# A hybrid mLSTM and convolution step: order of the decode queries, the state update, the next head's scores and the weight split

## The chip, the core and the metric

The kernel runs on one core of a Trainium2 chip. The time is the device time of one execution in microseconds (us). The engines are named as in the profile: PE is TensorE (matrix products), PEld its weight loads, DVE is VectorE, ACT is ScalarE, POOL is GpSimd and SP is SyncE, which here only issues DMAs. Each engine runs its own instructions in the order in which the program lists them, and waits for the others by semaphores.

## What is computed

One layer of a decoder in float32: 512 new tokens of a prompt and 8 samples of 8 tokens each, with width 2048. One projection feeds an mLSTM with four heads of 256 and a convolution group of 1024 channels; a second projection joins them, with a residual and a layer norm. The samples have a state each, 8 matrices C of 256 x 256 per head.

```python
proj = jnp.einsum('bsd,de->bse', x, w_in) + b_in
q, k, v, o, zm, ga, gg, zc, ig, fg = jnp.split(proj, SPLITS, axis=-1)
...
num = (w_inter[..., None] * jnp.einsum('bhtd,bhde->bhte', qc, C)
       + jnp.einsum('bhts,bhse->bhte', s, vc))
...
C_new = decay[..., None, None] * C + jnp.einsum('bhs,bhsd,bhse->bhde', ws, kc, vc)
...
out = jnp.einsum('bse,ed->bsd', mix, w_out)
y = _layernorm(DN_ALPHA * x.astype(jnp.float32) + out.astype(jnp.float32))
```

So the queries of the samples meet the old states C (first einsum of `num`), and the states are updated from the keys and values (`C_new`). The two are independent of each other but for C itself, which the update overwrites in place.

## The kernel before, in words

The projection is the backbone. It is cut into 61 steps (s = 4 to 64), one for every 128 output columns that are made there; a step has 16 slices (k) of 128 inputs, and a k is six matmuls: 576 tokens in two halves of 256 and 320 columns, times three products (whi by xh, whi by xl, wlo by xh) that together give float32 precision. Weights come in units of four k. A DMA brings 512 KB into a `raw` tile (two units); `split` (L77 to L91) makes from each unit a rounded part `whi` on ScalarE (L86) and the rest `wlo` on VectorE (L87). Both have RING = 4 tiles. In the main loop `split(u + RING - 1)` is called as unit u begins, so that three units stand ahead, and whi must wait until PE has left unit u - 1.

All other work is put beside the projection by a table: `at(s, k, f, ...)` lists what is emitted behind the matmuls of step s, slice k (a k of 16 or more runs on into the next step). Since every engine runs in order, this table fixes the order on each of them. For each head h, with b = 6 h + 1, these are, in order of the stage:

- `b_E` (L428 to L447): masks on POOL (L444), then exponentials on ScalarE (L439).
- `b_parts` (L455, L456) splits q and k in two; `b_QK` (L468 to L479) makes the scores; `b_rep`, `b_kT` (L502 to L507) and `b_stk` transpose k and lay it out for the samples; `b_q` (L482 to L492) lays the queries out in Q, in three bfloat16 parts. `b_vT` and what follows do the same for v.
- `c_split` (L379 to L407) cuts four states of the samples, one after the other, in three bfloat16 parts c0, c1, c2: c0 (L401) and c1 (L399) on ScalarE, the remainders cr (L407) and c2 (L404) on VectorE. It is done for two halves r of the 8 samples.
- `b_sKV(h, r)` (L646 to L658) makes four products of keys and values on PE (L652) and adds them to the decayed states in place on VectorE (L657); POOL sends each state out (`o_cs`, L658). `b_qC(h, r)` (L633 to L644) multiplies Q by the parts of the states (L640). `c_next` loads the next head's states into the tiles that are free.
- `b_sLN` (L664 to L680): part 0 is a product of the samples' own scores and values (L667), part 1 gathers the results of qC, part 2 adds them (L679) and calls `head_ln` (L600 to L622), whose root is two small activations (L594, L595). `b_shT` transposes the result.

Products of this side work share three PSUM tiles, `mi`, which are given out in turn: sKV takes all three and one more, and whoever comes next has to wait until VectorE has read one. For the projection there are other PSUM tiles (`pp`). At each step's end `evac` takes the step's result to SBUF (L201 to L203 for q, k, v).

In the convolution (steps after head 3's) VectorE adds 31 taps per channel (L766) for the prompt and reduces a window for the samples (L776, L778). The output projection (L1045 to L1080) takes its weights through the same ring.

Of the kernel before, what the change touches and what calls it, by code (L numbers as in the profile page):

```python
# [9 lines left out]
BF16 = mybir.dt.bfloat16  # L10
# [4 lines left out]
P = 128  # L15
# [29 lines left out]
NU_IN = 4 * len(ORDER)  # L45
NU_OUT = 56
NU_LAST = 8
NU = NU_IN + NU_OUT
RING = 4
EOFF = [0, 512, 896, 1152]  # L50
PAIRS = [(i, j) for i in range(4) for j in range(i + 1)]
CW = 410
# [4 lines left out]
def hybrid(ctx, tc, x0, wg0, wu, wgate, cpack, gpack, sct, hist, xres, lnp,  # L57
# [7 lines left out]
    def mt(shape, dt, name, tag=None, bufs=None):  # L65
        return main.tile(shape, dt, name=name, tag=tag or name, bufs=bufs or 1)
# [49 lines left out]
    hT = {}  # L116
# [150 lines left out]
    for k in range(KT):  # L267
        for n, x in enumerate((XH, XL)):
            for b in range(2):
                c0, c1 = SPANS[b]  # L270
                pe.matmul(pg[b][:40, :c1 - c0], lhsT=WG[k // 8][:, k % 8], rhs=x[k // 2][:, k % 2, c0:c1],
                          start=k == 0 and n == 0, stop=k == KT - 1 and n == 1)
    for n in range(3):
        split(n)
    G = [gt([40, TOK], F32R, n) for n in ("Gh", "Gl")]
    for ps, (c0, c1) in zip(pg, SPANS):
# [93 lines left out]
    m = {}  # L370
# [8 lines left out]
    def c_split(h, r, j, part):  # L379

        i = NB * h + 4 * r
        if (j, part) == (0, 0):
            if (h, r) == (0, 1):
                for n in ("c0", "c1"):
                    m[n] = [mt([P, 2, 2, 258], BF16, n, tag="hT", bufs=8) for _ in range(2)]
            else:
                for n, tag in (("c0", "Ph"), ("c1", "Pl")):
                    c = m["t"]([P, 4, 2, 258], BF16, n, tag=tag)  # L390
                    m[n] = [c[:, :2], c[:, 2:]]
            c = m["t"]([P, 4, 2, 258], BF16, "c2")
            m["c2"] = [c[:, :2], c[:, 2:]]
            m["cr"] = {}
        c0, c1, c2 = (lambda j, c=m[n]: c[j // 2][:, j % 2] for n in ("c0", "c1", "c2"))
        cr = m["cr"]
        if part == 0:
            if j:
                act.activation(c1(j - 1), cr[j - 1], AF.Copy)  # L399
            if j < 4:  # L400
                act.activation(c0(j), CS[i + j], AF.Copy)  # L401
        else:
            if j:
                dve.tensor_sub(c2(j - 1), cr.pop(j - 1), c1(j - 1))  # L404
            if j < 4:
                cr[j] = m["t"]([P, 2, 258], F32, "cr", bufs=2)
                dve.tensor_sub(cr[j], CS[i + j], c0(j))  # L407
# [285 lines left out]
    def at(s, k, f, *a):  # L693
        s, k = s + k // KT, k % KT
        beside.setdefault((s, k), []).append((f, a))
# [5 lines left out]
    for h in range(NH):  # L701
        b = 6 * h + 1
        o = 2 if h == 0 else 0
        for i in range(4):
            at(b + 3 + o, (14 + i if h == 0 else 7 + 2 * i), b_E, h, i)
        at(6 if h == 0 else b + 2, 11 if h == 0 else 5, b_parts, "q", h)
        at(6 if h == 0 else b + 4, 13 if h == 0 else 0, b_parts, "k", h)
        at(b + 4 + o, 5, b_QK, h, 0)
        at(b + 4 + o, 7, b_QK, h, 1)
        at(b + 4 + o, 7, b_rep, "k", h)  # L710
        at(b + 4 + o, 9, b_kT, h, 0)
        at(b + 4 + o, 11, b_kT, h, 1)
        at(b + 4 + o, 13, b_stk, "k", h)
        at(b + 4 + o, 14, b_q, h)
        if h + 1 < NH:
            at(b + 7, 0, rb_load, h + 1)
        o = 14 if h == 0 else 0
        at(b + 6, o + 1, b_rep, "v", h)
        at(b + 6, o + 2, b_vT, h, 0)
        at(b + 6, o + 4, b_vT, h, 1)  # L720
        at(b + 6, o + 6, b_stk, "v", h)
        at(b + 6, o + 7, b_vs, h)
        at(b + 6, o + 9, b_sn, h)
        o = (b + 6, o + 10)
        for I in range(4):
            at(o[0], o[1] + 2 * I, b_SV, h, I)
        at(o[0], o[1] + 7, lambda h: head_ln(m["num"], P, 4, CT[:, 14:18, h]), h)
        at(o[0], o[1] + 8, b_KV, h, 0)
        at(o[0], o[1] + 10, b_KV, h, 1)
        at(o[0], o[1] + 14, b_hT, h, 0)  # L730
        at(o[0], o[1] + 16, b_hT, h, 1)
        for r, k in enumerate((8, 30 if h == 0 else 29)):
            for j in range(5):
                for part in range(2):
                    at(o[0], o[1] + k + 4 * j + 2 * part, c_split, h, r, j, part)
            at(o[0], o[1] + (24, 49 if h == 0 else 46)[r], b_sKV, h, r)
            at(o[0], o[1] + (28, 51)[r], b_qC, h, r)
            at(o[0], o[1] + (33, 55)[r], c_next, h, r)
        at(o[0], o[1] + 26, b_sLN, h, 0)
        at(o[0], o[1] + 57, b_sLN, h, 1)  # L740
        at(o[0], o[1] + 66, b_sLN, h, 2)
        at(o[0], o[1] + 76, b_shT, h)


    cv = {}
# [170 lines left out]
    c0 = FIRST + ORDER.index(("zc", 0))  # L916
    c1 = c0 + 2
# [16 lines left out]
    for n_, (n, e) in enumerate(ORDER):  # L934
        s = FIRST + n_
        pp = pp_tile()
        outs = halves(pp[:, 0], pp[:, 1])
        for k in range(KT):
            u = 4 * n_ + k // 4
            if k % 4 == 0:  # L940
                split(u + RING - 1)
            w = slice((k % 4) * P, (k % 4 + 1) * P)
            proj(outs, WHI[u][:, w], WLO[u][:, w], k)
            for f, a in beside.pop((s, k), []):
                f(*a)
        evac(n, e, outs)
# [106 lines left out]
                (act if c0 > 1536 else nc.sync).dma_start(out[:, c0:c0 + 512 // n], zc)  # L1053

    blocks = [(0, 512), (512, 512), (1024, 512), (1536, 256), (1792, 256)]
    u, nxt = NU_IN, NU_IN + RING - 1
    act.preload_act_table_set("natural_log_exp_and_others")
    for bi, (c0, w) in enumerate(blocks):
        kpu = 512 // w
        pst = wo_tiles(bi)  # L1060
        if bi < 4:
            for un in range(KT // kpu):
                for _ in range(2):
                    if nxt < NU and nxt <= u + RING - 1 or NU <= nxt < NU + NU_LAST:
                        split(nxt)
                        nxt += 1
                mix_next(2)
                if bi < 2 and un > 1 and extra:
                    nc.sync.dma_start(*extra.pop(0))
                for kk in range(kpu):  # L1070
                    kt = un * kpu + kk
                    hi, lo = (W[u][:, kk * w:(kk + 1) * w] for W in (WHI, WLO))
                    for t in range(5):
                        wmm(pst[t][:, :w], t, kt, hi, lo)
                u += 1
            later = [evac_z(t, pst[t], c0, w) for t in range(5)]
            while bi == 3 and nxt < NU + NU_LAST:
                split(nxt)
                nxt += 1
            for f in later:  # L1080
                f()
        else:
            for t in (4, 0, 1, 2, 3):
                for kt in range(KT):
                    hi, lo = (W[:, kt * w:(kt + 1) * w] for W in lastw)
                    wmm(pst[t][:, :w], t, kt, hi, lo)
                f = evac_z(t, pst[t], c0, w)
                f()
                ln_ops(t)
# [58 lines left out]
```

## Time and profile before

| | |
|---|---|
| time, median of 3 runs | 1145.81 us (1145.46 to 1146.2) |
| the profiled execution | 1146.47 us |
| its span | 1144.8 us |
| mean granted TensorE clock | 0.992 |
| PE busy | 1120.3 us (98%) |
| PEld busy | 1072.1 us (94%) |
| DVE busy | 740.9 us (65%) |
| ACT busy | 424.4 us (37%) |
| POOL busy | 148.6 us (13%) |

The span is the time from the first to the last instruction that the profiler saw; the execution's own time has a little around it. Busy shares are means over stages that differ: ScalarE and VectorE are half idle over the whole program, and can still be late in one place. Where a row of the timeline ends in brackets, the engine was idle for the first number of us just before, and the name is that of the instruction that ended it. A granted clock of 1.00 is 2.4 GHz, and 0.5 would be 1.2 GHz all through.

### The profile page before, as it was taken

How to read it: one execution, taken by the hardware profiler on the slowest of the kernel's cores; microseconds unless marked ns; L12 is line 12 of the kernel's file. 1: busy time of each engine (PE TensorE's matmuls, PEld its weight loads, DVE VectorE, ACT ScalarE, POOL GpSimd, SP SyncE). 2: the span in 40 equal slices, each digit the busy share in tenths (PEclk: the TensorE clock that was granted, in tenths of full speed). 3: DMA queues.
4: the chain of work that ended last, by engine and by line, in shares of the span. 5: the costliest groups of instructions: out<-in, count | busy, mean ns of one | idle time of the engine just before them, and what ended most of it. 6: DMA issues, size and time to landing. Idle time of an engine off the chain costs nothing.

```text
span 1144.8 us, 19958 instructions
## 1 busy us (share of the span) xinstructions
PE 1120.3 (98%) x8126; PEld 1072.1 (94%) x8126; DVE 740.9 (65%) x1250; ACT 424.4 (37%) x813; POOL 148.6 (13%) x217
## 2 busy tenths in 40 slices
PE   9999999999999998999999999999999999999996
PEld 8999998989999997999999999999999988888896
DVE  6385555555465545527899898999977871433448
ACT  5335553454445454422222222221336661221224
POOL 0021021021021002200011111111203310000004
PEclk9999999999999998999999999999999999999998
DMA  8114244244235222332233223222232245542228
GB/s 292 68 56 160 84 142 146 79 145 146 74 113 197 80 66 93 110 108 92 84 107 102 90 85 100 75 74 92 79 107 74 77 156 186 199 153 94 65 93 166
DMA packets 45228, 129.09 MB, mean 113 GB/s; under 512 B 5660, under 2 KB 11164, under 8 KB 44688
## 3 DMA queue, kind: packets, MB, share of 16 engines
q1 hardware_dynamic: 38880, 113.11, 29.6%
q0 software_dynamic: 4992, 12.94, 4.3%
q10 hardware_dynamic: 1264, 1.78, 0.5%
q8 instruction: 63, 1.03, 0.4%
q14 instruction: 29, 0.24, 0.1%
HBM read 110.91 MB, written 19.78 MB: 114 GB/s over the span
## 4 chain that ended last, share of the span: by engine, by line
PE 60%; DVE 1%; issue 0%; DVEq 0%
PE pp L185 42%; PE pp L1020 3%; PE pp L1021 3%; PE pp L1019 3%; PE mi L1020 2%; PE mi L1021 2%; PE mi L1019 2%; PE mi L1016 1%; PE mi L1015 1%; PE ns L1021 0%; PE ns L1019 0%; PE ns L1020 0%; DVE Ct L657 0%; DVE z L1052 0%; DVE c L404 0%; DVE z L1040 0%
## 5 line engine op out<-in xcount | busy, mean ns | idle before, releaser
L185 PE MATMUL pp<-xh,whi 128*128 128x256 f32 (+1 forms) x1952 | 422.8, 298 | 0.0
L185 PE MATMUL pp<-xl,whi 128*128 128x256 f32 (+1 forms) x1952 | 416.6, 295 | 0.0
L185 PE MATMUL pp<-xh,wlo 128*128 128x256 f32 (+1 forms) x1952 | 416.2, 295 | 0.0
L87 DVE TENSOR_TENSOR wlo<-raw,whi 128x512 fp32r<-128x512 f32 x300 | 220.8, 740 | 278.6 <-ACT whi L86 278.4
L185 PEld LDWEIGHTS pp<-xh,whi 128*128 128x128 f32 x1952 | 324.0, 189 | 5.2 <-issue 3.7
L185 PEld LDWEIGHTS pp<-xh,wlo 128*128 128x128 f32 x1952 | 327.6, 189 | 0.0
L185 PEld LDWEIGHTS pp<-xl,whi 128*128 128x128 f32 x1952 | 327.3, 189 | 0.0
L86 ACT ACTIVATE whi<-raw 128x512 fp32r<-128x512 f32 x300 | 187.6, 631 | 335.3 <-PE pp L185 175.8
L766 DVE SCALAR_TENSOR_TENSOR Y<-U,cp,Y 128x512 f32<-128x512 f32 x240 | 189.7, 790 | 5.3
L1020 PE MATMUL pp<-whi,mx 128*128 128x512 f32 (+1 forms) x128 | 46.9, 366 | 0.0
L1019 PE MATMUL pp<-whi,mx 128*128 128x512 f32 (+1 forms) x128 | 46.9, 366 | 0.0
L1021 PE MATMUL pp<-wlo,mx 128*128 128x512 f32 (+1 forms) x128 | 46.9, 366 | 0.0
L658 POOL DMA_DIRECT2D o_cs<-Ct x32 | 22.7, 779 | 170.8 <-DVE Ct L657 170.6
L1020 PE MATMUL mi<-whi,mx 128*128 128x512 f32 (+1 forms) x96 | 36.1, 376 | 0.0
L1019 PE MATMUL mi<-whi,mx 128*128 128x512 f32 (+1 forms) x96 | 36.0, 375 | 0.0
L1021 PE MATMUL mi<-wlo,mx 128*128 128x512 f32 (+1 forms) x96 | 36.0, 375 | 0.0
L399 ACT ACTIVATE c<-cr 128x516 bf16<-128x516 f32 x32 | 20.2, 632 | 42.0 <-DVE cr L407 42.0
L799 ACT ACTIVATE sg<-pp,cp 128x256 f32<-128x256 f32 (+1 forms) x48 | 21.3, 495 | 38.3 <-PE pp L185 38.2
L1021 PEld LDWEIGHTS pp<-wlo,mx 128*128 128x128 f32 x128 | 24.1, 188 | 4.3
L1019 PEld LDWEIGHTS pp<-whi,mx 128*128 128x128 f32 x128 | 24.0, 188 | 4.3
L1020 PEld LDWEIGHTS pp<-whi,mx 128*128 128x128 f32 x128 | 24.0, 188 | 4.3
L1047 POOL DMA_DIRECT2D o_ys<-zs x4 | 3.4, 1182 | 188.9 <-ACT zs L1046 188.9
(340 smaller groups left out, 1378.6 us busy)
## 6 DMA issues: line engine op xcount, KB each, us to landing
raw<-wu SPq DMA_DIRECT2D x154, 512.0 KB
Ct<-sct SPq DMA_DIRECT2D x32, 258.0 KB
o_cs<-Ct POOLq DMA_DIRECT2D x32, 256.0 KB, 3.2
xr<-x SPq DMA_DIRECT2D x16, 288.0 KB
z<-xres SPq DMA_DIRECT2D x8, 512.0 KB
wr<-wg SPq DMA_DIRECT2D x16, 192.0 KB
o_y<-z POOLq DMA_DIRECT2D x11, 256.0 KB, 7.0
o_y<-lnp SPq DMA_DIRECT2D x2, 1024.0 KB
```

The source lines that it names most:

```text
L86: act.activation(hi, r, AF.Copy)
L87: (eng or dve).tensor_tensor(out=lo, in0=r, in1=hi, op=OP.subtract)
L185: pe.matmul(out[b], lhsT=w, rhs=x[:, slice(*SPANS[b])], start=k == 0 and n < 2, stop=k == KT - 1 and n >= 4)
L399: act.activation(c1(j - 1), cr[j - 1], AF.Copy)
L658: pool.dma_start(o_cs[NB * h + b], c)
L766: dve.scalar_tensor_tensor(y, u, w, y, op0=OP.mult, op1=OP.add)
L799: act.activation(sg[:, c0:c1], ps, AF.Sigmoid, bias=b_in[:, c:c + 1])
L1015: pe.matmul(ps, lhsT=s_, rhs=hi, start=first, stop=False)
L1016: pe.matmul(ps, lhsT=s_, rhs=lo, start=False, stop=last)
L1019: pe.matmul(ps, lhsT=h_, rhs=hi, start=first, stop=False)
L1020: pe.matmul(ps, lhsT=l_, rhs=hi, start=False, stop=False)
L1021: pe.matmul(ps, lhsT=h_, rhs=lo, start=False, stop=last)
```

## The change

The numbers of the `at` table and the lead of the weight split are changed; no instruction of arithmetic is added or taken away.

- `LEAD = RING - 2`: units are split two ahead, at the start, in the main loop and in the output projection. RING stays 4.
- The order in each half r of the states was sKV, then qC, then c_next. It is now qC (21 k behind the first part of c_split), sKV (23) and c_next (27). For heads above 0 the second c_split begins one k later. The three parts of sLN move by one k, shT too.
- For h = 1 the group parts(k), QK, rep(k), kT, stk(k), q is emitted 16 to 17 k later, for h = 2 and 3 it is 4 k later.
- `c_split(0, 1)` uses the tiles Ph and Pl, as the other calls do, and two tiles of its own are gone.

```diff
@@ -47,6 +47,7 @@
 NU_LAST = 8
 NU = NU_IN + NU_OUT
 RING = 4
+LEAD = RING - 2
 EOFF = [0, 512, 896, 1152]
 PAIRS = [(i, j) for i in range(4) for j in range(i + 1)]
 CW = 410
@@ -270,7 +271,7 @@
                 c0, c1 = SPANS[b]
                 pe.matmul(pg[b][:40, :c1 - c0], lhsT=WG[k // 8][:, k % 8], rhs=x[k // 2][:, k % 2, c0:c1],
                           start=k == 0 and n == 0, stop=k == KT - 1 and n == 1)
-    for n in range(3):
+    for n in range(LEAD):
         split(n)
     G = [gt([40, TOK], F32R, n) for n in ("Gh", "Gl")]
     for ps, (c0, c1) in zip(pg, SPANS):
@@ -379,16 +380,11 @@
     def c_split(h, r, j, part):
 
 
-
         i = NB * h + 4 * r
         if (j, part) == (0, 0):
-            if (h, r) == (0, 1):
-                for n in ("c0", "c1"):
-                    m[n] = [mt([P, 2, 2, 258], BF16, n, tag="hT", bufs=8) for _ in range(2)]
-            else:
-                for n, tag in (("c0", "Ph"), ("c1", "Pl")):
-                    c = m["t"]([P, 4, 2, 258], BF16, n, tag=tag)
-                    m[n] = [c[:, :2], c[:, 2:]]
+            for n, tag in (("c0", "Ph"), ("c1", "Pl")):
+                c = m["t"]([P, 4, 2, 258], BF16, n, tag=tag)
+                m[n] = [c[:, :2], c[:, 2:]]
             c = m["t"]([P, 4, 2, 258], BF16, "c2")
             m["c2"] = [c[:, :2], c[:, 2:]]
             m["cr"] = {}
@@ -704,14 +700,15 @@
         for i in range(4):
             at(b + 3 + o, (14 + i if h == 0 else 7 + 2 * i), b_E, h, i)
         at(6 if h == 0 else b + 2, 11 if h == 0 else 5, b_parts, "q", h)
-        at(6 if h == 0 else b + 4, 13 if h == 0 else 0, b_parts, "k", h)
-        at(b + 4 + o, 5, b_QK, h, 0)
-        at(b + 4 + o, 7, b_QK, h, 1)
-        at(b + 4 + o, 7, b_rep, "k", h)
-        at(b + 4 + o, 9, b_kT, h, 0)
-        at(b + 4 + o, 11, b_kT, h, 1)
-        at(b + 4 + o, 13, b_stk, "k", h)
-        at(b + 4 + o, 14, b_q, h)
+        at(6 if h == 0 else b + 4, 13 if h == 0 else 17 if h == 1 else 4, b_parts, "k", h)
+        o = 16 * o + (0, 16, 4, 4)[h]
+        at(b + 4, o + 5, b_QK, h, 0)
+        at(b + 4, o + 7, b_QK, h, 1)
+        at(b + 4, o + 7, b_rep, "k", h)
+        at(b + 4, o + 9, b_kT, h, 0)
+        at(b + 4, o + 11, b_kT, h, 1)
+        at(b + 4, o + 13, b_stk, "k", h)
+        at(b + 4, o + 14, b_q, h)
         if h + 1 < NH:
             at(b + 7, 0, rb_load, h + 1)
         o = 14 if h == 0 else 0
@@ -729,17 +726,17 @@
         at(o[0], o[1] + 10, b_KV, h, 1)
         at(o[0], o[1] + 14, b_hT, h, 0)
         at(o[0], o[1] + 16, b_hT, h, 1)
-        for r, k in enumerate((8, 30 if h == 0 else 29)):
+        for r, k in enumerate((8, 30)):
             for j in range(5):
                 for part in range(2):
                     at(o[0], o[1] + k + 4 * j + 2 * part, c_split, h, r, j, part)
-            at(o[0], o[1] + (24, 49 if h == 0 else 46)[r], b_sKV, h, r)
-            at(o[0], o[1] + (28, 51)[r], b_qC, h, r)
-            at(o[0], o[1] + (33, 55)[r], c_next, h, r)
-        at(o[0], o[1] + 26, b_sLN, h, 0)
-        at(o[0], o[1] + 57, b_sLN, h, 1)
-        at(o[0], o[1] + 66, b_sLN, h, 2)
-        at(o[0], o[1] + 76, b_shT, h)
+            at(o[0], o[1] + k + 21, b_qC, h, r)
+            at(o[0], o[1] + k + 23, b_sKV, h, r)
+            at(o[0], o[1] + k + 27, c_next, h, r)
+        at(o[0], o[1] + 25, b_sLN, h, 0)
+        at(o[0], o[1] + 58, b_sLN, h, 1)
+        at(o[0], o[1] + 67, b_sLN, h, 2)
+        at(o[0], o[1] + 77, b_shT, h)
 
 
     cv = {}
@@ -938,7 +935,7 @@
         for k in range(KT):
             u = 4 * n_ + k // 4
             if k % 4 == 0:
-                split(u + RING - 1)
+                split(u + LEAD)
             w = slice((k % 4) * P, (k % 4 + 1) * P)
             proj(outs, WHI[u][:, w], WLO[u][:, w], k)
             for f, a in beside.pop((s, k), []):
@@ -1053,7 +1050,7 @@
                 (act if c0 > 1536 else nc.sync).dma_start(out[:, c0:c0 + 512 // n], zc)
 
     blocks = [(0, 512), (512, 512), (1024, 512), (1536, 256), (1792, 256)]
-    u, nxt = NU_IN, NU_IN + RING - 1
+    u, nxt = NU_IN, NU_IN + LEAD
     act.preload_act_table_set("natural_log_exp_and_others")
     for bi, (c0, w) in enumerate(blocks):
         kpu = 512 // w
@@ -1061,7 +1058,7 @@
         if bi < 4:
             for un in range(KT // kpu):
                 for _ in range(2):
-                    if nxt < NU and nxt <= u + RING - 1 or NU <= nxt < NU + NU_LAST:
+                    if nxt < NU and nxt <= u + LEAD or NU <= nxt < NU + NU_LAST:
                         split(nxt)
                         nxt += 1
                 mix_next(2)
```

The first place is VectorE from the end of c_split(0, 0) on, in step 10. L657 is the update of sKV (L653 after the change), L404 makes c2 (L400), L407 makes cr (L403), L87 is wlo (L88). Before:

```order
L87 TENSOR_TENSOR wlo<-raw,whi 128x512
L657 SCALAR_TENSOR_TENSOR Ct<-Ct,dec,mi 128x2x256 x3
L657 SCALAR_TENSOR_TENSOR Ct<-Ct,dec,ns 128x2x256
L404 TENSOR_TENSOR c_1719<-cr,c_1718 128x516
L87 TENSOR_TENSOR wlo<-raw,whi 128x512 x2
L407 TENSOR_TENSOR cr<-Ct,c_1987 128x516
L87 TENSOR_TENSOR wlo<-raw,whi 128x512
L404 TENSOR_TENSOR c_1991<-cr,c_1989 128x516
L407 TENSOR_TENSOR cr<-Ct,c_1987 128x516
```

and after the change:

```order
L88 TENSOR_TENSOR wlo<-raw,whi 128x512
L400 TENSOR_TENSOR c_1713<-cr,c_1712 128x516
L88 TENSOR_TENSOR wlo<-raw,whi 128x512
L653 SCALAR_TENSOR_TENSOR Ct<-Ct,dec,mi 128x2x256 x3
L653 SCALAR_TENSOR_TENSOR Ct<-Ct,dec,ns 128x2x256
L88 TENSOR_TENSOR wlo<-raw,whi 128x512
L403 TENSOR_TENSOR cr<-Ct,c_1963 128x516
L88 TENSOR_TENSOR wlo<-raw,whi 128x512
L400 TENSOR_TENSOR c_1965<-cr,c_1964 128x516
```

The update stood ahead of the last c2 of the first half; it now stands behind it, next to the first cr of the second half.

The second place is ScalarE at the end of step 12 after the change, from kT of head 1 to the evacuation of v. There kwh is the transposed and weighted k, sm the root of head norm in sLN(0, 2), hi the replicated k, Q the queries. The same part for head 1 in the kernel before (at the end of step 11):

```order
L506 ACTIVATE kwh<-mi,CT 128x256 x2
L642 ACTIVATE nsb<-mi 128x258
L644 DMA nsd_719<-nsb 128x516
L506 ACTIVATE kwh<-mi,CT 128x256 x2
L86 ACTIVATE whi<-raw 128x512
L542 ACTIVATE hi<-mi,WSs 128x256 x2
L489 ACTIVATE Q<-qw 128x16x8
L491 ACTIVATE Q<-qw 128x16x8
L203 ACTIVATE v<-pp,cp 128x256
L203 ACTIVATE v<-pp,cp 128x320
```

and after the change:

```order
L502 ACTIVATE kwh<-mi,CT 128x256 x2
L590 ACTIVATE sm_2437<-sm_2437 64x1
L591 ACTIVATE sm_2437<-sm_2437 64x1
L502 ACTIVATE kwh<-mi,CT 128x256 x2
L87 ACTIVATE whi<-raw 128x512
L538 ACTIVATE hi<-mi,WSs 128x256 x2
L485 ACTIVATE Q<-qw 128x16x8
L487 ACTIVATE Q<-qw 128x16x8
L204 ACTIVATE v<-pp,cp 128x256
L204 ACTIVATE v<-pp,cp 128x320
```

Before, the small activations of sLN(0, 2) came later, behind the evacuation of v; now they stand between the second and the third kwh, and what follows them is the end of step 12, not of step 11. The qC result (nsb) is gone from between the kwh.

## Rows read from the trace of the kernel before

**Rows 1.** The page, part 1: each engine's busy time, share of the span, instructions.

```profile
PE 1120.3 (98%) x8126; PEld 1072.1 (94%) x8126; DVE 740.9 (65%) x1250; ACT 424.4 (37%) x813; POOL 148.6 (13%) x217
```

**Rows 2.** What PE waits for, whole span: us in total, times, longest us.

```profile
PE mi L667 <- DVE Ct L657: 6.4, 3, 4.8
PE mi L640 <- DVE c L404: 3.1, 5, 1.2
```

**Rows 3.** Timeline of PE at three gaps: start us, us, row, [idle before <-releaser].

```profile
176.92 0.66 PE L502 MATMUL mi<-ident,k 128*128 128x128 f32 x4 [2.37 <-DVE Ct L657]
...
439.11 1.12 PE L667 MATMUL mi<-vs,Es 64*64 64x258 f32 x2 [4.82 <-DVE Ct L657]
...
465.00 0.52 PE L640 MATMUL mi<-c,Q 128*32 128x258 bf16 x12 [1.17 <-DVE c L404]
```

**Rows 4.** Stretches behind two gaps: us, then busy PE, PEld, DVE, ACT, POOL; PEclk, DMA.

```profile
175.00:184.00 9.00, 7.08 (x61) 6.40 (x62) 5.36 (x10) 2.47 (x6) 3.46 (x6) 0.81 0.76 237
436.00:444.00 8.00, 4.89 (x34) 3.71 (x38) 6.24 (x8) 1.53 (x3) 4.06 (x5) 0.57 0.58 196
```

**Rows 5.** The convolution: a stretch of 20 us; timelines of DVE and PE.

```profile
780.00:800.00 20.00, 20.00 (x154) 20.00 (x153) 19.61 (x26) 3.95 (x7) 1.42 (x1) 1.00 0.24 83
...
804.56 0.68 DVE L87 TENSOR_TENSOR wlo<-raw,whi 128x512 fp32r<-128x512 f32 x1
...
845.74 2.70 DVE L87 TENSOR_TENSOR wlo<-raw,whi 128x512 fp32r<-128x512 f32 x3 [0.94 <-ACT whi L86]
...
876.20 1.57 DVE L87 TENSOR_TENSOR wlo<-raw,whi 128x512 fp32r<-128x512 f32 x1 [1.33 <-ACT whi L86]
...
802.64 0.42 PE L185 MATMUL pp<-xh,whi 128*128 128x256 f32 x2
...
843.72 0.42 PE L185 MATMUL pp<-xh,whi 128*128 128x256 f32 x2
```

**Rows 6.** Head 0 to head 1: timelines of PE, DVE, POOL, ACT; L468 alone, 165 to 174.

```profile
147.32 0.39 PE L652 MATMUL mi<-vS,kS 32*128 32x256 f32 x3
...
155.15 0.42 PE L185 MATMUL pp<-xh,whi 128*128 128x256 f32 x2
...
150.67 0.74 DVE L657 SCALAR_TENSOR_TENSOR Ct<-Ct,dec,ns 128x512 f32<-128x512 f32 x1
...
152.30 2.16 POOL L444 TENSOR_TENSOR E<-RB,cmask 128x128 f32<-128x128 f32 x4
...
155.68 0.39 ACT L439 ACTIVATE E<-E,CT 128x128 f32<-128x128 f32 x1
...
sum 9.00, PE 4.26 PEld 3.58; mean PE 2.13 PEld 1.79
```

**Rows 7.** Timeline of ACT, three rows of one turn of c_split, head 3.

```profile
423.74 0.64 ACT L399 ACTIVATE c<-cr 128x516 bf16<-128x516 f32 x1 [2.05 <-DVE cr L407]
...
424.80 0.62 ACT L86 ACTIVATE whi<-raw 128x512 fp32r<-128x512 f32 x1
...
427.39 0.63 ACT L399 ACTIVATE c<-cr 128x516 bf16<-128x516 f32 x1 [0.82 <-DVE cr L407]
```

**Rows 8.** Timelines of PE and ACT behind kT of head 0, ACT in sLN(1,2).

```profile
114.52 0.60 PE L520 MATMUL mi<-ident,v 128*128 128x128 f32 x4
...
113.67 0.87 ACT L203 ACTIVATE q<-pp,cp 128x256 f32<-128x256 f32 x2
...
285.81 0.20 ACT L594 ACTIVATE sm<-sm 64x1 f32<-64x1 f32 x1 [3.63 <-DVE sm L617]
```

**Rows 9.** Timelines of DVE and ACT, c_split of head 3, third and fourth state.

```profile
435.90 1.89 DVE L404 TENSOR_TENSOR c<-cr,c 128x516 bf16<-128x516 f32 x1
...
438.43 0.63 ACT L399 ACTIVATE c<-cr 128x516 bf16<-128x516 f32 x1 [3.50 <-DVE cr L407]
```

**Rows 10.** Timelines of DVE and PE, a unit's wlo and its first matmul, head 2.

```profile
291.69 1.29 DVE L87 TENSOR_TENSOR wlo<-raw,whi 128x512 fp32r<-128x512 f32 x2 [1.01 <-ACT whi L86]
...
293.57 0.43 PE L185 MATMUL pp<-xh,whi 128*128 128x256 f32 x2
```

## Prediction

> **What bounds the kernel now.** TensorE does. The busy line of the page has PE at 98% of the span [rows 1], and the view of what engines wait for, asked for PE, finds 11.9 us in the middle of the program: 6.4 us in L667 (the samples' own scores) and 3.1 us in L640 (queries meet the states) [rows 2], and 2.4 us in L502 (transpose of k) [rows 3]. In the timeline these are nine gaps, eight of 0.3 to 2.4 us and one of 4.82 us; three stand in [rows 3]. Then comes the clock. In the stretches behind the gaps of 2.37 and 4.82 us the granted clock falls to a mean of 0.81 and 0.57 [rows 4], that is to 1.2 GHz for part of the time: 9.0 x (1 - 0.81) x 2 = 3.4 us and 8.0 x (1 - 0.57) x 2 = 6.9 us, of which the last 2.2 us of the stall itself cost nothing. Half of the rest is lost: 1.7 + 2.3 = 4.0 us. Behind the gap of 1.17 us [rows 3] the clock stayed whole. So 11.9 + 4.0 = **15.9 us** is all that better placed work can win. Everything else that I count is a new wait of PE.
>
> The span is 1144.8 us and the profiled execution took 1146.47 us; the sum is made against that. The median of the runs is 1145.81 us, 0.66 us less, and the end result is brought to it.
>
> **Units used below.** One k of the projection is six matmuls. Thirteen units of four k lie between 802.64 and 843.72 [rows 5]: 3.16 us a unit, 0.79 us a k. PE first reads a unit's wlo two thirds into its first k, 0.53 us after the unit starts.
>
> **What goes away.** All 15.9 us is taken as gone at first, and what is late next is then put in its place. The L667 stalls go because sKV, whose VectorE work (L657) must empty the mi banks before L667 can have one, now comes after both sLN and qC, with a long run of plain projection behind it. The L502 stall goes because no kT follows sKV any more. The L640 stalls of heads 1 and 2 go because qC stands three k behind the last part of c_split, not one to three with the split still in hand. L640's last one (head 3, second half) goes for the same reason. Two edits I cost at nothing: c_split(0,1) now writes Ph and Pl, which qC(0,0) has read one k before, and c_next stands two k later on SP's queue, where the next reader of its Ct tiles is a whole head away. If that cover were gone, a late Ct would hold ScalarE's c0, which is the chain of A and D.
>
> **Term A, head 0 to head 1.** sKV(0,0) moves from the end of k 0 of step 10 to the end of k 7, just ahead of E(1,0), and on POOL the four o_cs DMAs stand ahead of E as they did. PE ran sKV at 147.32; the new place is 155.15 less the 0.44 us that sKV itself took earlier, so 7.4 us later [rows 6]. The first L657 was held up some 0.7 us by a wlo there, which will be done by now, so the L657 end moves 6.6 us: the fourth from 150.67 to 157.3. POOL's E came 1.63 us behind the fourth L657 (152.30) [rows 6] and had no other need, so it comes at 158.9, its first quarter (0.54 us) is ready at 159.5, and the first exp on ScalarE, which ran at 155.68, waits 3.8 us. Queued behind that exp on ScalarE are c1 and c0 of c_split(0,1) and every whi. c1 of the first state can run at 160.9 (four exps of the first row take 1.4 us). One turn c1, c0, whi on ScalarE, wlo, c2, cr on VectorE took 3.66 us (c1 at 423.74 and again at 427.39 [rows 7]), more than a unit. Three turns are 11.0 us, the other exps and the two evacuations of k in them some 2.0, and from the last c1 over whi and wlo to the end of c2 2.3: c2 of the fourth state is ready at about 176.2. PE used to be idle from 174.55 (176.92 - 2.37 [rows 3]); in the new order QK (4.26 us [rows 6]) and sKV (0.44) no longer stand before that point, and qC(0,1) comes two k behind it: PE arrives at 171.4. **Stall 4.8 us**; bounds 3 (if the exps slip in between) and 6.
>
> **Term B, end of step 12.** With k, QK, kT and q of head 1 sixteen k later, the evacuation of v's second half at the end of step 12 stands on ScalarE behind four kwh, two hi, two Q and now also behind the two small activations (L594, L595) of sLN(0,2). In head 0 the same row without head LN shows how tight this is: the evacuation ends at 113.67 + 0.87 = 114.54, and PE is at vT, the reader of v, at 114.52 [rows 8]. Head LN's VectorE chain made ScalarE wait 3.63 us before its first small activation, which with its twin takes 0.34 [rows 8]. So the evacuation ends 4.0 us behind PE. **Stall 4.0 us**; bounds 2 (part of head LN runs before kT) and 5.
>
> **Term C, heads 2 and 3.** QK to q move 4 k on and fall behind sLN(h,2). In the old order the wlo pair at 291.69 had its first half done at 292.4 and PE began that unit at 293.57 [rows 10], 1.7 us of slack counted to the wlo's first use. With two units ahead a unit's split stands one unit, 3.16 us, later, of which the shorter queue gives back some 0.3. **1.2 us each, 2.4 in all**; bounds 0 and 3.
>
> **Term D, head 3, first half.** PE came to L667 at 434.29 (439.11 - 4.82 [rows 3]). sKV leaves, qC follows three k later: arrival near 437.0. The c_split chain there does not depend on what is moved: it hangs on the evacuation of z_m, for which ScalarE loads a table. c2 of the third state began at 435.90 and took 1.89 us, and c1 of the fourth ran at 438.43 [rows 9]. Behind it come whi and wlo (0.6 and 0.7) and c2 (0.7): ready at 441.2. **Stall 4.2 us** in place of 4.82; bounds 2 and 5.5. The 1.89 us stand against 0.69 elsewhere for the same form, while POOL multiplied hT. The Trainium skill, SBUF — State Buffer, section "SBUF: two separate sides", says that an operation of VectorE with two SBUF inputs and one of GpSimd that reads SBUF lock each other out; the row agrees. If they should not meet in the new order, D would be 1.2 us less.
>
> **Term E, weights two ahead.** Where VectorE has slack this costs nothing: the cover is the two units of projection that remain between split and use. In the convolution VectorE has none: it is busy 19.61 of 20 us [rows 5], so its instructions keep their times, and each wlo slot then serves the unit before the one it served. The wlo at 804.56 ends at 805.24; the unit that now stands there starts at 802.64 and wants it at 803.17 [rows 5]: 2.1 us late. Two slots on it is 2.8. Of the three wlo from 845.74 to 848.44, 0.6 each at the end, the first ends at 847.24; the unit now there starts at 843.72 and wants it at 844.25 [rows 5]: 3.0 us late, and the delays are not added but the largest counts. After 860 VectorE waits for PE again, and the slow wlo at 876.20 (1.57 us) [rows 5], done at 877.8 for a unit that would start at 875.9, adds 1.5. **4.5 us**; bounds 2 and 6. In the output projection the smallest slack is over one unit: nothing.
>
> **Term F, the clock.** A, B and D are each longer than the 2.37 us that cost the clock and the 1.17 that did not. At 2.0 us each, the mean of the two prices above: **6.0 us**; bounds 0 and 7.
>
> **Sum.** 4.8 + 4.0 + 2.4 + 4.2 + 4.5 + 6.0 = 25.9 us come, 15.9 go: +10.0. 1146.47 + 10.0 - 0.66 = **1155.8 us**.
>
> **Rivals.** (1) *Faster: the ring was the brake.* Each whi waits for PE to leave a slot; with two ahead the slot is long empty, and whi, exps, c0 and c1 run early. It decides if the turn of 3.66 us shrinks below the unit's 3.16: with 2.5 us a turn, A falls to 1.3 and D to 1.2 without a clock drop; B with its drop (6.0) and 3.0 in the convolution stay: 11.5 - 15.9 = -4.4, **1141.4 us**. Against it: in the loop whi at 424.80 had no wait at all and c1 waited for cr [rows 7], so the turn is its own circle and not PE's. For it: ScalarE's whi does wait for PE in quieter stretches.
> (2) *The clock holds.* All stalls come, none costs the clock: 19.9 - 15.9 = +4.0, **1149.8 us**. The Trainium skill, TensorE: Matmul & The Clock Gate, Part 1, says that the gate judges activity in windows that run free of the program; by that the same stall may or may not trip it. For the drop: both gaps above 2 us tripped it [rows 4].
> (3) *No price for the shorter lead.* VectorE enters the convolution a unit ahead, since no whi holds it, and E is nothing: +5.5, **1151.3 us**. Against: a queue that is busy 98% wins nothing by an early start at one end.
> (4) *They cancel.* 2 and 3 together, -0.5, **1145.3 us**.
>
> **Chances.** Forecast 0.53, (1) 0.13, (2) 0.14, (3) 0.12, (4) 0.08. No more than 2 in 10 may lie outside: the range takes in (2) to (4) and the better half of (1), and above it B, C and E at their upper bounds with 1.0 more of clock (+5), plus 1.2 on A: **1142.5 to 1162**. 0.2% is 2.3 us, about what a measurement of this kernel can tell from no change. Faster is (1), 0.13; the same is (4), 0.08; slower the rest, 0.79.
>
> **What would show it.** Right: no wait of L667 for L657, a PE gap of 4 to 5 us ahead of L640 (now L636) near 171 and again near 437, one ahead of vT near 200, a few of 1 to 3 us on wlo near 803 and 844, and a granted clock below 1 behind the long ones. Wrong: c_split turns below 3.16 us, L640 never waiting, or wlo of the convolution ready a unit early.

## The result, and the profile after

| | before | after |
|---|---|---|
| median of the runs | 1145.63 us (1144.42 to 1146.2) | 1155.83 us (1154.27 to 1157.23) |
| the profiled execution | 1146.47 us | 1154.27 us |
| its span | 1144.8 us | 1152.3 us |

The change makes the kernel slower: the ratio is 1.009, with a 95% interval of 1.0073 to 1.0108. The forecast was 1155.8 us. The hit to a tenth of a microsecond is partly luck: the profiled execution is 7.8 us slower than its counterpart, and a second comparison of the same kernel gave 1.0069 (1.0056 to 1.0082).

The busy line of the page after the change, beside [rows 1], is as full as before, over a longer span:

```profile
PE 1124.7 (98%) x8126; PEld 1074.0 (93%) x8126; DVE 743.1 (64%) x1250; ACT 417.7 (36%) x813; POOL 151.9 (13%) x217
```

What PE waits for after the change (us in total, times, longest), beside [rows 2]. No wait for L653, the state update, is left. The waits for c1 (L395), for v and for weights are new; the wait for c2 (L400) was there before (as L404), at other places:

```profile
PE mi L636 <- ACT c L395: 4.3, 2, 2.3
PE mi L516 <- ACT v L204: 4.0, 1, 4.0
PE mi L636 <- DVE c L400: 3.4, 2, 1.8
...
PE pp L186 <- DVE wlo L88: 1.5, 3, 0.8
PE pp L186 <- ACT whi L87: 1.2, 3, 0.7
```

The timeline of PE at the three long waits, beside [rows 3]. qC(0,1) and qC(3,0) wait twice each, first for c1 and then for c2, vT of head 1 once:

```profile
173.38 0.29 PE L636 MATMUL mi<-c,Q 128*32 128x258 bf16 x4 [2.28 <-ACT c L395]
...
175.23 0.96 PE L636 MATMUL mi<-c,Q 128*32 128x258 bf16 x13 [1.56 <-DVE c L400]
...
206.28 0.90 PE L516 MATMUL mi<-ident,v 128*128 128x128 f32 x3 [3.99 <-ACT v L204]
...
443.35 0.29 PE L636 MATMUL mi<-c,Q 128*32 128x258 bf16 x4 [2.02 <-ACT c L395]
...
445.47 1.02 PE L636 MATMUL mi<-c,Q 128*32 128x258 bf16 x13 [1.83 <-DVE c L400]
```

The stretches behind these waits, beside [rows 4]. The eighth number, PEclk, is 0.79 each time, so each stretch of 8 us holds 8.0 x 0.21 x 2 = 3.4 us at 1.2 GHz. Half of that is lost, less what fell in the end of the wait itself: 1.7, 1.6 and 1.4 us, 4.7 in all:

```profile
172.00:180.00 8.00, 5.06 (x40) 4.13 (x40) 3.03 (x6) 2.17 (x4) 0.00 (x0) 0.79 0.35 117
204.00:212.00 8.00, 5.72 (x32) 5.49 (x33) 4.37 (x8) 4.06 (x11) 0.69 (x5) 0.79 0.41 131
444.00:452.00 8.00, 6.53 (x51) 5.75 (x51) 4.37 (x7) 2.03 (x5) 1.33 (x3) 0.79 0.23 72
```

The steps that led to the first two waits, beside [rows 6] and [rows 8]: POOL's masks, the first exp behind them, the end of the chain (c2 of the fourth state), and the evacuation of v:

```profile
157.98 2.16 POOL L440 TENSOR_TENSOR E<-RB,cmask 128x128 f32<-128x128 f32 x4
...
158.91 0.40 ACT L435 ACTIVATE E<-E,CT 128x128 f32<-128x128 f32 x1 [5.30 <-POOL E L440]
...
174.49 0.69 DVE L400 TENSOR_TENSOR c<-cr,c 128x516 bf16<-128x516 f32 x1
...
205.77 0.88 ACT L204 ACTIVATE v<-pp,cp 128x256 f32<-128x256 f32 x2
```

The exp has waited 5.30 us for POOL; c2 ends at 175.18, PE had come at 171.09. The row of v holds two pieces: the first, begun at 205.77, lets PE go at 206.28, and PE had come at 202.29.

The convolution, beside [rows 5], where PE now waits for weights:

```profile
770.40 0.53 PE L186 MATMUL pp<-xh,wlo 128*128 128x256 f32 x2 [0.40 <-DVE wlo L88]
...
805.79 0.54 PE L186 MATMUL pp<-xh,whi 128*128 128x256 f32 x2 [0.74 <-ACT whi L87]
...
806.91 0.53 PE L186 MATMUL pp<-xh,wlo 128*128 128x256 f32 x2 [0.32 <-DVE wlo L88]
...
882.55 0.53 PE L186 MATMUL pp<-xh,wlo 128*128 128x256 f32 x2 [0.80 <-DVE wlo L88]
```

### The profile page after: what moved, and what is told of

It is laid out like the page before. It is cut to its first block, busy times and chain, and to the rows that moved or that the text cites. A ratio compares the mean times of both kernels' runs of the same rounds, so it can differ in the third digit from the quotient of the medians.

```text
span 1152.3 us, 19908 instructions
## 1 busy us (share of the span) xinstructions
PE 1124.7 (98%) x8126; PEld 1074.0 (93%) x8126; DVE 743.1 (64%) x1250; ACT 417.7 (36%) x813; POOL 151.9 (13%) x217
## 4 chain that ended last, share of the span: by engine, by line
PE 78%; DVE 10%; issue 7%; ACT 4%; POOL 1%; DMA 1%; DVEq 0%; ACTq 0%; POOLq 0%; SPq 0%
PE pp L186 53%; PE pp L1018 3%; PE pp L1016 3%; PE pp L1017 3%; PE mi L1017 2%; PE mi L1018 2%; PE mi L1016 2%; DVE wlo L88 2%; DVE Y L763 2%; PE mi L1013 1%; PE mi L1012 1%; PE mi L186 1%; PE mi L464 1%; ACT whi L87 1%; PE mi L574 1%
## 5 line engine op out<-in xcount | busy, mean ns | idle before, releaser
L88 DVE TENSOR_TENSOR wlo<-raw,whi 128x512 fp32r<-128x512 f32 x300 | 221.5, 745 | 234.4 <-ACT whi L87 234.2
L87 ACT ACTIVATE whi<-raw 128x512 fp32r<-128x512 f32 x300 | 183.1, 629 | 239.2 <-PE mi L1012 91.8
L395 ACT ACTIVATE c<-cr 128x516 bf16<-128x516 f32 x32 | 20.2, 632 | 37.0 <-DVE cr L403 37.0
L653 DVE SCALAR_TENSOR_TENSOR Ct<-Ct,dec,mi 128x512 f32<-128x512 f32 x24 | 16.5, 745 | 23.3 <-PE ns L648 22.8
L1016 PEld LDWEIGHTS pp<-whi,mx 128*128 128x128 f32 x128 | 24.0, 188 | 4.3
```

The lines of the kernel that those rows point to most:

```text
L87: act.activation(hi, r, AF.Copy)
L88: (eng or dve).tensor_tensor(out=lo, in0=r, in1=hi, op=OP.subtract)
L653: dve.scalar_tensor_tensor(c, c, m["dec", h][:, b:b + 1], pss[j], op0=OP.mult, op1=OP.add)
L1016: pe.matmul(ps, lhsT=h_, rhs=hi, start=first, stop=False)
```

## The experiments

Each kernel stands beside runs of the kernel before on the same chip (e: 1147.55 us, f: 1146.9 us, g: 1147.25 us, medians), and kernels of different letters are compared by their ratios to these. A gap is PE's idle time in the timeline.

### One part alone: the lead

**e1.** With three units ahead again, all else as changed:

```diff
-LEAD = RING - 2
+LEAD = RING - 1
```

> The changed kernel with weights split three units ahead again (LEAD = RING - 1), all else as changed. Theory (the shorter lead costs some 5 us in the convolution and under 1 us a head, three reordered places the rest): the gaps of PE on whi and wlo between 298 and 883 us go, those at 171, 202 and 441 us stay; PE starts its first step 0.8 us later. 5.3 + 1.5 - 0.8 = 6.0 us less than the changed kernel, near 1150 us (1148 to 1152). Rival 1, the shorter lead is the whole loss: 1145.6 us, and the head gaps shrink too. Rival 2, the lead costs nothing because VectorE is the limit there whatever its order: 1155.8 us.

Measured: 1148.74 us, 1.0014 of the kernel before (1.0004 to 1.0024). The gaps on weights are gone, those at 171, 202 and 440 us are there (2.71 + 1.56, 4.00, 2.01 + 1.72 us). So all that the change does to the order of work costs some 1.6 us, and the lead the rest of 1.009 or of the control's 1.0069: 6 to 9 us.

**e2.** The other way round, the kernel before with the lead alone:

```diff
-                split(u + RING - 1)
+                split(u + RING - 2)
```

and the same number at the start and in the output projection.

> The kernel before with weights split two units ahead and nothing else changed. Theory: the same convolution loss as in the changed kernel, 5.3 us, one more at the two units that had 1.7 us of slack in heads 2 and 3 (up to 2.9 us together), less 0.8 us at the start: 1145.6 + 5 to 7 = 1151 to 1153 us; the old head gaps (L667, L640, L502) stay as they were. Rival 1, the lead is the whole loss: 1155.8 us. Rival 2, a shorter lead frees ScalarE from the ring and shortens the old head gaps as much as it costs: 1145 to 1147 us.

Measured: 1154.26 us, 1.0067 (1.0051 to 1.0083), 7.7 us. The waits of PE in it; the first and the third are those of [rows 2], unmoved, and the second and the last are the price of the lead. The wait of L502, forecast to stay at 2.37 us, fell to 1.71, and the granted clock behind it stayed at 1.00 where it had been 0.81 [rows 4]; so in this profiled execution the lead took some 2 us more than the difference of the times says:

```profile
PE mi L667 <- DVE Ct L657: 6.4, 3, 4.8
PE pp L185 <- ACT whi L86: 3.2, 3, 1.2
PE mi L640 <- DVE c L404: 3.1, 5, 1.2
...
PE pp L185 <- DVE wlo L87: 1.5, 3, 0.8
```

Two of the L86 waits are in heads 2 and 3:

```profile
289.65 0.53 PE L185 MATMUL pp<-xh,whi 128*128 128x256 f32 x2 [1.18 <-ACT whi L86]
...
389.35 0.53 PE L185 MATMUL pp<-xh,whi 128*128 128x256 f32 x2 [1.17 <-ACT whi L86]
```

They are 1.2 us each, the size that term C had, but at the units that begin at 290.39 and 388.44 us in the kernel before, each one unit ahead of the one that term C looked at (293.57 in head 2). In the changed kernel it is that next unit that waits, and only 0.25 us (298 and 395 us). That the later scores give ScalarE the room is likely, but no run moves them alone. Judged by its time alone, e2 cannot be told from the control of the changed kernel (1.0067 and 1.0069): net, the lead is nearly the whole loss, since what the new order takes away and what it brings nearly cancel (e1). As an account of the waits both rivals still fall: the old head gaps cost as much as ever but for L502, and the new ones stay without the lead (e1).

### The three waits in the heads, one at a time

**e3.** POOL's masks of head 1 ahead of the output DMAs of the first update:

```diff
-(14 + i if h == 0 else 7 + 2 * i), b_E, h, i)
+(14 + i if h == 0 else 6 if (h, i) == (1, 0) else 7 + 2 * i), b_E, h, i)
```

> The changed kernel with POOL's masks of head 1 (first part of E) emitted one k earlier, so that they stand ahead of the four output DMAs of the first state update instead of behind them. Theory (the exps wait 5.3 us for POOL's masks, and c_split behind them on ScalarE makes PE wait 3.85 us at the first qC(0,1), which costs the clock too): the exps start near 153.5 us instead of 158.9, the gap near 171 us falls to 1.5 us or less and the clock stays whole there: 3.5 to 5 us less, 1151 to 1152.5 us. Rival, the turn of c_split (3.66 us) alone makes it late, POOL does not matter: a gap of 3 us or more stays, 1155 us or more.

Measured: 1153.77 us, 1.0057 (1.0041 to 1.0073). That is 1.4 us less than the second ratio of the changed kernel (the control, below), whose interval overlaps, and 3.8 less than the first. Neither side has it whole: the gap went from 3.84 to 2.53 us, between the 1.5 of the theory and the 3 of the rival.

```profile
172.89 0.29 PE L636 MATMUL mi<-c,Q 128*32 128x258 bf16 x4 [0.97 <-ACT c L395]
...
174.75 1.02 PE L636 MATMUL mi<-c,Q 128*32 128x258 bf16 x13 [1.56 <-DVE c L400]
```

The exps now start at 154.70 instead of 158.91, and c1 of the first state still comes only at 159.59: it waits for cr, and the first cr of c_split(0,1) stands on VectorE behind the state update.

```profile
157.54 0.74 DVE L653 SCALAR_TENSOR_TENSOR Ct<-Ct,dec,ns 128x512 f32<-128x512 f32 x1
...
158.81 0.69 DVE L403 TENSOR_TENSOR cr<-Ct,c 128x516 f32<-128x516 f32 x1
...
159.59 0.64 ACT L395 ACTIVATE c<-cr 128x516 bf16<-128x516 f32 x1 [3.62 <-DVE cr L403]
```

So POOL's place set 1.3 us of the lateness. Behind it the moved update is the next brake, on VectorE, and from the first c1 to the end of the last c2 c_split takes 15.1 us as in the changed kernel. And the clock, which the theory had whole, fell here too, behind two gaps of 0.97 and 1.56 us with 0.29 us of work between them:

```profile
168.00:176.00 8.00, 5.47 (x53) 4.36 (x52) 3.73 (x6) 3.03 (x6) 0.00 (x0) 0.92 0.21 68
176.00:184.00 8.00, 8.00 (x58) 7.70 (x57) 5.07 (x8) 3.79 (x8) 3.84 (x6) 0.87 0.57 194
```

**e4.** Part 2 of the sample norm of head 0 behind the evacuation of v:

```diff
-at(o[0], o[1] + 67, b_sLN, h, 2)
-at(o[0], o[1] + 77, b_shT, h)
+at(o[0], o[1] + (72 if h == 0 else 67), b_sLN, h, 2)
+at(o[0], o[1] + (82 if h == 0 else 77), b_shT, h)
```

> The changed kernel with part 2 of the sample layer norm of head 0 five k later, behind the evacuation of v (and its transpose back five k later too). Theory (head norm between the second and third kwh on ScalarE delays the evacuation of v by 4 us, and PE waits for it): the gap of 3.99 us ahead of vT at 202 us goes, with 1.6 us of clock: 5.6 us less, 1150.2 us (1149 to 1152). Rival, head norm only moves the wait (vh or the replicated v behind it are late): a gap of 2 us or more turns up between 203 and 215 us, 1153 to 1156 us.

Measured: 1151.1 us, 1.0041 (1.0027 to 1.0055), 5.6 us less than the changed kernel by the first ratio and 3.2 by the control's. The gap of 3.99 us is gone, and a smaller one stands at the transposed v, 1.61 us, which head norm on VectorE now delays. Its clock stayed at 1.00:

```profile
210.04 0.41 PE L551 MATMUL mi<-ident,v 128*64 128x128 f32 x2 [1.61 <-DVE vl L519]
```

```profile
200.00:208.00 8.00, 8.00 (x63) 7.88 (x63) 5.28 (x17) 2.67 (x9) 0.69 (x5) 1.00 0.22 68
208.00:216.00 8.00, 6.39 (x50) 5.93 (x49) 5.74 (x14) 4.31 (x11) 0.00 (x0) 1.00 0.20 66
```

The cause of the wait at 202 us is shown; the place chosen for head norm was not yet the best.

**f1.** The states of head 3 six k later:

```diff
-for r, k in enumerate((8, 30)):
+for r, k in enumerate((8, 36 if h == 3 else 30)):
+    d = 6 if (h, r) == (3, 0) else 0
...
-at(o[0], o[1] + k + 21, b_qC, h, r)
+at(o[0], o[1] + k + 21 + d, b_qC, h, r)
```

and the same 6 k for sKV and c_next of the first half and for parts 1 and 2 of sLN and shT of head 3; `open_c`, which opens the tiles of the convolution, is called five k later (30, 15).

> The changed kernel with the states of head 3 alone moved: qC and the update of the first half six k later, the second half six k later as a whole. Theory (the chain of c_split there hangs on the evacuation of z_m and is 3.9 us late for PE, whatever comes): the gap of 2.03 + 1.83 us near 441 us goes, and 1.5 us of clock with it: 5.4 us less than the changed kernel. Rival, the wait moves to the second half (its c_split begins six k later too): a gap of 1.5 us or more near 468 us and under 4 us gained.

Measured: 1158.8 us, 1.0101 (1.0087 to 1.0115), 3.6 us *more* than the control beside it. The gap near 441 us did go, as the theory had it, and the rival took more than it gave: the second half now met the evacuation of z_m of the next step.

```profile
468.61 0.29 PE L636 MATMUL mi<-c,Q 128*32 128x258 bf16 x4 [1.32 <-ACT c L395]
...
472.85 1.02 PE L636 MATMUL mi<-c,Q 128*32 128x258 bf16 x13 [3.94 <-DVE c L400]
```

### Only the order of the states, and the control

**f0.** The changed kernel once more, without an edit:

> The changed kernel itself once more, as the control of this call: 1.009 of the kernel before, as measured, so 1155 to 1158 us. Theory: the same gaps to 0.1 us (3.85 us near 171, 4.0 near 202, 3.86 near 441, 2.3 together on whi and wlo from 768 to 883 us).

Measured: 1155.18 us, 1.0069 (1.0056 to 1.0082), with the gaps of the changed kernel to 0.15 us (2.30 + 1.55, 4.00, 2.00 + 1.83; weights 0.24 to 0.87).

**f2.** The kernel before with the new order of qC, sKV and c_next alone:

```diff
-for r, k in enumerate((8, 30 if h == 0 else 29)):
+for r, k in enumerate((8, 30)):
...
-at(o[0], o[1] + (24, 49 if h == 0 else 46)[r], b_sKV, h, r)
-at(o[0], o[1] + (28, 51)[r], b_qC, h, r)
-at(o[0], o[1] + (33, 55)[r], c_next, h, r)
+at(o[0], o[1] + k + 21, b_qC, h, r)
+at(o[0], o[1] + k + 23, b_sKV, h, r)
+at(o[0], o[1] + k + 27, c_next, h, r)
```

and sLN and shT one k apart from before, as in the change.

> The kernel before with only the order of the state work changed as in the change (qC, then sKV, then c_next; the second half one k later), three units ahead and the next heads' scores where they were. Theory (this part of the change takes the L667 and L640 waits away, 7 us of them outside head 3's 4.82): those of heads 1 and 2 go (5 us), head 3 keeps some 4 us near 437, the last L640 wait of 1.17 us goes, and head 0 has a gap of 2 to 5 us at qC(0,1), since the masks come late here too: 2 to 6 us less than the kernel before. Rival, without the later scores the new order meets kT and QK in the mi banks and is slower: 2 us or more above the kernel before.

Measured: 1148.74 us, 1.0007 (0.9996 to 1.0018): no difference that can be told. Theory and rival both miss. What follows is read from a profiled execution of 1152.29 us, 3.5 us above that median. The L667 and L640 waits of heads 1 and 2 do go, and four new ones in head 0 to head 1 take their place, at QK (2.00 and 1.28 us, late kh and kl), sKV and stk; and the wait for v is there although kT is not beside it:

```profile
168.81 0.50 PE L468 MATMUL mi<-qh,kh 128*128 128x512 f32 x1 [2.00 <-ACT kh L455]
...
206.83 0.20 ACT L594 ACTIVATE sm<-sm 64x1 f32<-64x1 f32 x1 [10.97 <-DVE sm L617]
...
208.20 0.55 PE L520 MATMUL mi<-ident,v 128*128 128x128 f32 x3 [3.95 <-ACT v L203]
```

ScalarE sat 10.97 us before the root of head norm. VectorE was waiting for the gathered results of qC, and that DMA (n) stands on SP's queue behind the four loads of Ct. These stand behind a load of weights (raw), which waited 12.8 us for VectorE's wlo, until 193.69; once it was out, the loads of Ct followed at once, and the issues of n waited 3.5 us more for them. The first two lines are what SP's queue waits for from 175 to 212 us:

```profile
SPq L75 <- DVE wlo L87: 31.5, 3, 12.8
SPq L675 <- DMA Ct<-sct: 3.5, 4, 1.3
...
180.51 13.51 SPq L75 DMA_DIRECT2D raw<-wu  x2
...
194.11 1.81 SPq L377 DMA_DIRECT2D Ct<-sct  x4
...
195.97 5.97 SPq L675 DMA_DIRECT2D n<-nsd  x8
```

In the kernel before the loads of Ct were issued from 179.85, ahead of that load of weights, the load of weights at 189.87 and the gathering from 190.25. The prediction had costed c_next's place on that queue at nothing; behind the load of weights, where f2 has it, it is not nothing. In both kernels it is head norm standing ahead of the evacuation of v that makes PE wait for v.

### A version without the waits

**f3.** Those edits together, with three units ahead, the masks one k earlier and head 3 six k later as above, qC(0,1) four k later and head norm of head 0 eight (sKV and c_next of that half, the gathering and shT go along):

```diff
-LEAD = RING - 2
+LEAD = RING - 1
...
+d = 6 if (h, r) == (3, 0) else 4 if (h, r) == (0, 1) else 0
...
-at(o[0], o[1] + 67, b_sLN, h, 2)
+at(o[0], o[1] + (73 if h == 3 else 75 if h == 0 else 67), b_sLN, h, 2)
```

> The changed kernel with three units ahead, the masks of head 1 one k earlier, qC(0,1) four k later, part 2 of the sample norm of head 0 eight k later, and head 3's states six k later. Theory (four separate waits, each undone by its own edit): no gap over 1 us in the heads and a whole clock: 4.3 + 1.7, 4.0 + 1.6 and 3.7 + 1.5 us less than with three units ahead alone (1.0014 of the kernel before), so 0.987 to 0.990 of the kernel before, 11 to 15 us less. Rival, work that is moved late only meets the next stage: gaps of 1 to 4 us turn up behind the old ones and no more than 6 us is won against the kernel before.

Measured: 1139.88 us, 0.9939 (0.9926 to 0.9951), 7.0 us less than the kernel before. In heads 0 to 2 no gap over 0.24 us is left; head 3 has the 1.33 + 3.94 us of f1. So the theory, 11 to 15 us, missed, and the rival had the gaps right and the gain nearly (6 us at most).

**g1.** Head 3's states were then put back and its first c_split made tighter, so that it is ahead of the z_m evacuation on ScalarE:

```diff
+q = 3 * j + part if (h, r) == (3, 0) else 4 * j + 2 * part
-at(o[0], o[1] + k + 4 * j + 2 * part, c_split, h, r, j, part)
+at(o[0], o[1] + k + q, c_split, h, r, j, part)
```

> As f3_all_mended, but head 3's states stay where the change put them, and its first c_split is emitted in three k a state instead of four, so that it stands ahead of the evacuation of z_m on ScalarE. Theory (what made f3 lose is that its second half met the next z_m evacuation, 1.3 + 3.9 us of gap and the clock): no gap over 1 us anywhere, so 5.3 + 1.5 us less than f3: 0.987 to 0.990 of the kernel before. Rival, the turn of c_split (3.66 us) is too slow for three k a state and a gap of 2 us or more stays ahead of the first qC of head 3: 0.990 to 0.994.

Measured: 1132.0 us, **0.9865 of the kernel before (0.9851 to 0.9878), 15.2 us less**; it beats both kernels. That is close to the 15.9 us that the prediction counted as what better placed work can win, and a little more than the forecast for this run. All that the view of PE's waits lists in it:

```profile
PE ns L221 <- DVE warm L218: 1.5, 1, 1.5
PE mi L464 <- DVE kl L452: 0.2, 1, 0.2
PE mi L558 <- ACT vs L552: 0.2, 1, 0.2
```

**g2.** The same with two units ahead:

```diff
-LEAD = RING - 1
+LEAD = RING - 2
```

> g1_head3_tighter with weights split two units ahead. Theory (the price of the lead is paid in the convolution, a stage that the heads do not reach): 5 to 7 us above g1, with the same gaps on whi and wlo between 750 and 880 us (some 2.3 us by the rows, more by the shift of later steps). Rival, the price was paid where the heads' waits delayed ScalarE, and goes with them: within 2 us of g1.

Measured: 1138.18 us, 0.9918 (0.9904 to 0.9931), 6.2 us above g1. The waits on weights are those of the changed kernel:

```profile
PE pp L186 <- DVE wlo L88: 1.5, 3, 0.8
PE pp L186 <- ACT whi L87: 1.2, 3, 0.7
```

So the price of the lead does not hang on the heads' waits, and the rival falls.

### The clock by itself

**g3.** The changed kernel with matmuls in the gaps, 26 ahead of qC(0,1) and of qC(3,0), and, by two more lines of the same kind that are left out here, 27 ahead of vT:

```diff
+for _ in range({(0, 1): 26, (3, 0): 26}.get((h, r), 0)):
+    pe.matmul(ps[:, :256], lhsT=ones, rhs=XH[0][:, 0, :256], start=True, stop=True)
```

> The changed kernel with 26, 27 and 26 matmuls of 256 columns (0.13 us each) put on PE ahead of qC(0,1), the first vT of head 1 and qC(3,0), into the tile that the next matmul overwrites: they add work that no output uses, in time that PE would have waited. Theory (the three gaps cost 4.7 us of clock beside their own length): granted clock 1.00 near 176, 208 and 446 us, 3.5 to 4.7 us less than the changed kernel (0.9969 of it or lower). Rival, the clock's price is small or falls for another reason: within 1.5 us of the changed kernel.

Measured: 1151.82 us, 1.0035 (1.0023 to 1.0048), against 1.0069 of the control and 1.009 at first: 3.9 to 6.3 us less, though more work was added; the intervals do not meet. The granted clock:

```profile
176.00:184.00 8.00, 7.97 (x72) 7.46 (x72) 5.29 (x8) 4.00 (x8) 4.08 (x7) 1.00 0.58 197
208.00:216.00 8.00, 8.00 (x64) 7.75 (x63) 3.59 (x7) 3.53 (x8) 0.00 (x0) 1.00 0.20 69
444.00:452.00 8.00, 8.00 (x65) 7.70 (x65) 5.92 (x9) 3.94 (x9) 2.83 (x4) 1.00 0.57 181
```

So the three waits cost about as much again in clock as one of them lasts: 4.7 us by the rows of the result, 3.9 to 6.3 by this run.

## Why the prediction was right, point by point

- **What goes.** As forecast: no wait for the update is left, nor any of the L640 waits of heads 1 and 2 and of head 3's second half. Those are the 11.9 us of gaps and 4.0 of clock of [rows 2 to 4].
- **Term A**, 4.8 us forecast, 3.84 measured. POOL's masks at 157.98 (forecast 158.9), the exp at 158.91 (159.5), c2's end at 175.18 (176.2), PE's arrival at 171.09 (171.4). All steps of the chain stood; each was up to 1 us too late. But the chain has a second brake just behind the first, which the prediction did not name: the moved update holds VectorE until 157.1, so that cr of the first state ends at 158.57, and c1, which ran at 160.10, could not run before that whatever POOL does. e3 shows its weight: without POOL's delay only 1.3 of the 3.84 us go.
- **Term B**, 4.0 forecast, 3.99 measured. e4 shows the cause. That it is right to 0.01 us is luck: the row that was to show how tight the evacuation and vT are without head norm is of q (113.67, [rows 8]), which vT does not read. e4 shows it instead: there the first piece of v, begun at 202.50, is in time for PE.
- **Term C**, 2.4 forecast. The step that failed: that the split stands one unit later while the queue gives back 0.3 us. In the changed kernel the gaps are 0.25 us each, and the steps behind each are put back by 0.7 us, as in g2 (last section). Gaps of 1.2 us came only in e2, one unit earlier; what gives the room back in the changed kernel stays open.
- **Term D**, 4.2 forecast, 3.85 measured, at 441.32 (437.0 forecast plus the 4.3 us by which PE was late by then). The slow c2 that was weighed there came again, at 440.11 with 1.92 us, while POOL multiplied hT from 439.74 to 441.48. It agrees with the Trainium skill, SBUF — State Buffer, section "SBUF: two separate sides", on the lock between VectorE and GpSimd.
- **Term E**, 4.5 forecast. From the first k of step 33 to the last of step 64 PE took 404.85 us before and 410.12 after, 5.3 us more (4.8 in e2 against before, 4.3 in g2 against g1). Two of the three places were forecast, 805 and 882; at 844 it was 0.14 us, since PE had fallen back enough by then, as "the largest counts" says; 770 was not forecast.
- **Term F**, 6.0 forecast, some 4.7 measured. All three waits cost the clock, but what one of them costs is not fixed: the wait near 441 us cost half as much low clock in this profile as in those of e1 and e3 (last section). With that agrees the Trainium skill, TensorE: Matmul & The Clock Gate, Part 1, by which the windows of the gate run free of the program.
- **Sum.** 3.84 + 3.99 + 0.5 + 3.85 + 5.3 + 4.7 = 22.2 us come, 15.9 go: +6.3, where the profiled executions differ by 7.8 us. The rest is 0.5 us more behind the last matmul, and gaps on weights that shift the steps by more than their length (last section). The forecast of +10.0 oversized A, C, D and F by 4.5 us and undersized E by 0.8; that the medians gave +10.2 was in its favour, since the control gave some 8.
- **Rival 1** (the ring was the brake) falls: two units ahead shorten the gap at qC(0,1) by 0.4 us against three (e1) and not by 3.5, the turn of c_split is 3.66 us as before (c1 at 169.04 and 172.70), and ScalarE waits there for POOL and cr. **Rival 2** (the clock holds) falls by the rows, **rival 3** (no price for the lead) by e1, e2 and g2, and **rival 4**, which needs both, with them.
- **Not run alone** are the later scores and the tiles Ph and Pl for c_split(0,1). In the trace after, the first c0 there follows at 152.47 right behind the result of qC(0,0), without a wait of its own, so the tiles cost nothing at that place, as forecast.

## What to carry to other kernels

Where engines run in order, an instruction's lateness is read from what stands ahead of it on its own engine, and the sum of a change is made place by place: old waits that go, then for each moved piece the time at which its inputs are ready against the time at which the bottleneck arrives. A wait removed is not a gain until the next one behind it is known: the same reordering was worth nothing as it stood, and 15 us once the late pieces (masks, head norm, a state split, the weight lead) had been given other places. In the convolution here, with VectorE busy 98% of the stage and 65% of the span, the shorter lead cost 4.3 to 5.3 us.

## What the runs showed of the hardware that was not expected

- A gap on weights costs more than its row. Between g1 and g2, where only the lead differs, the gap of 0.78 us at 866 us shifts the next k by 1.16 us, that of 0.39 at 755 by 0.65, and those of 0.25 us (289 and 386) by 0.7 each. The seven gaps on weights in g2 are 2.9 us in all, and from the first step to the end of the projection g2 takes 5.8 us longer than g1.
- The clock does not follow the length of one gap. It fell behind 0.97 + 1.56 us with 0.29 us of work between (e3), and it held behind 1.71 us (e2), 1.61 us (e4), 1.17 us (before) and 0.97 us (g3). Whether two near gaps count as one, or the place in the program decides, no run here tells apart.
- The same wait does not always cost the same. At qC(3,0) PE waits 2.02 + 1.83 us in the changed kernel and 2.03 + 1.83 us in e3, but from 440 to 452 us the granted clock is 0.86 in the one and 0.72 in the other, which is 12 x 0.14 x 2 = 3.4 us and 12 x 0.28 x 2 = 6.7 us at 1.2 GHz. The control and e4 have 0.86 there too, e1 has 0.72. Half of the difference, 1.7 us, is what two profiles can differ by at one and the same wait. The first line is of the changed kernel, the second of e3:

```profile
440.00:452.00 12.00, 8.15 (x70) 6.74 (x69) 7.00 (x10) 3.37 (x7) 2.80 (x4) 0.86 0.15 48
440.00:452.00 12.00, 8.14 (x60) 6.54 (x59) 6.19 (x9) 3.37 (x7) 2.00 (x3) 0.72 0.14 44
```
